# A streamed multiply-and-GELU: the stretch of DRAM loaded first and stored last goes from 5 KB rows to 16 KB rows

## The chip, the cores and the metric

The kernel runs on one core of a Trainium2 chip. The metric is the device time of one execution in microseconds (us), the median of several runs. The engines that matter here are VectorE (DVE in the profile), ScalarE (ACT), SyncE (SP), which issues nearly all transfers, and the 16 DMA engines, which move all bytes between DRAM and the on-chip memory SBUF.

## The reference

Two arrays of 1024 x 4096 float32 are multiplied, and the tanh form of GELU is taken of the product. Each element is independent of all others.

```python
z = x * y
return 0.5 * z * (1 + tanh(sqrt(2 / pi) * (z + 0.044715 * z ** 3)))
```

Each array has 16.78 MB, so 33.55 MB are read and 16.78 MB are written. The kernel computes in float32 throughout.

## The kernel before

**Layout.** SBUF has 128 partitions. The kernel looks at each array as one flat run of 4,194,304 elements and deals out 32,768 of them to each partition. An element keeps no fixed place in a matrix: since the operation is elementwise, any assignment will do as long as x, y and out use the same one. The flat run is cut into three stretches, `PIECES` (line 14). Within a stretch of w columns the helper `columns` (line 51) gives partition p the w consecutive elements that begin at p * w. One transfer therefore moves 128 rows, each contiguous in DRAM, and the row length is 4 * w bytes: 5,120 bytes for the stretch of 1,280 columns, 65,536 for 16,384 columns and 60,416 for 15,104 columns. I call the stretches S (small, first in DRAM), M (middle) and L (last).

**Buffers.** `xs` holds all 32,768 columns of x; products and results overwrite it in place. `ys` holds only 20,440 columns (`Y_BUF`, line 22), so y comes in three loads that share the room. `Y_LOADS` (line 16) lists them as (first column, end, place in `ys`): M at 4056, then L at 0, then S at 15104. Loads L and S overwrite places that products over M must have read before, and `Y_FREE` (line 18) says how many products must be done: 3 for L, 4 for S.

**Order of the transfers.** x of S is issued by SP and x of M by ScalarE's queue, both placed ahead of the kernel's opening barrier by `_hoist` (lines 79 and 80). SP then waits until x of S has landed (line 81) and issues y of M and x of L. It waits for three products and issues y of L, waits for four and issues y of S (lines 84 to 87). After that come the three stores, M, L and S, in the loop at line 111. Each waits until ScalarE has finished its last column (line 114); the first one also waits for a further semaphore (line 113), before: the landing of y of L. All of SP's transfers go through one queue in the order of issue; ScalarE's queue has the one load of x of M. All transfers of both queues share the same 16 DMA engines.

**Compute.** VectorE multiplies in the order of `Y_LOADS`, in steps of `STEPS` (line 20): four steps of 4,096 columns over M, seven of 2,048 and one of 768 over L, one of 1,280 over S. Ahead of the first step of each stretch it waits for the landing of that stretch of x and of y (lines 92 to 95). Each step is followed by one ScalarE activation over the same columns (line 106), which waits for that step (line 105). `done` keeps the number of the step that ends at a column, and line 114 uses it.

**End.** SP waits for the first two stores, clears the semaphores, and waits for the last store (lines 116 to 121).

Of the kernel before, what the change touches and what calls it, by code (L numbers as in the profile page):

```python
# [1 line left out]

# [4 lines left out]

F32 = mybir.dt.float32
GELU = mybir.ActivationFunctionType.Gelu_apprx_tanh  # L10

PIECES = [(0, 1280), (1280, 17664), (17664, 32768)]

Y_LOADS = [(1280, 17664, 4056), (17664, 32768, 0), (0, 1280, 15104)]

Y_FREE = [0, 3, 4]

STEPS = [[4096] * 4, [2048] * 7 + [768], [1280]]  # L20
STORES = [(1280, 17664), (17664, 32768), (0, 1280)]
Y_BUF = 20440

def _hoist(nc, issued):

    here = nc.cur_bb.bb.instructions
    first = nc.main_func.blocks[0].instructions
    for ins in issued:
        del here[next(k for k, i in enumerate(here) if i is ins or i.name == ins.name)]  # L30
    engine = issued[0].engine
    at = next(
        k
        for k, i in enumerate(first)
        if i.engine == engine and type(i).__name__ == "InstDrain"
    )
    first[at:at] = issued

@with_exitstack  # L40
def kernel(
    ctx: ExitStack,
    tc: tile.TileContext,
    x: bass.AP,
    y: bass.AP,
    out: bass.AP,
):
    nc = tc.nc
    P = nc.NUM_PARTITIONS

    def columns(t, a, b):

        flat = t.flatten_outer_dims().rearrange("r c -> (r c)")
        pa, pb = next(q for q in PIECES if q[0] <= a and b <= q[1])
        return flat[P * pa : P * pb].rearrange("(p c) -> p c", p=P)[:, a - pa : b - pa]

    tc.close()
    tc.compile()  # L59

    xs = nc.alloc_sbuf_tensor("xs", [P, PIECES[-1][1]], F32).ap()
    ys = nc.alloc_sbuf_tensor("ys", [P, Y_BUF], F32).ap()
    sem_x = [nc.alloc_semaphore(f"sem_x{i}") for i in range(len(PIECES))]
    sem_y = [nc.alloc_semaphore(f"sem_y{i}") for i in range(len(Y_LOADS))]
    sem_mul = nc.alloc_semaphore("sem_mul")
    sem_act = nc.alloc_semaphore("sem_act")
    sem_o = [nc.alloc_semaphore(f"sem_o{i}") for i in range(len(STORES))]

    def load_x(i, engine=nc.sync):
        a, b = PIECES[i]  # L70
        return engine.dma_start(out=xs[:, a:b], in_=columns(x, a, b)).then_inc(sem_x[i], 16)

    def load_y(i):
        a, b, r = Y_LOADS[i]
        return nc.sync.dma_start(
            out=ys[:, r : r + b - a], in_=columns(y, a, b)
        ).then_inc(sem_y[i], 16)

    _hoist(nc, [load_x(0).ins])
    _hoist(nc, [load_x(1, nc.scalar).ins])  # L80
    nc.sync.wait_ge(sem_x[0], 16)
    load_y(0)
    load_x(2)
    for i in range(1, len(Y_LOADS)):
        if Y_FREE[i]:
            nc.sync.wait_ge(sem_mul, Y_FREE[i])
        load_y(i)

    n = 0
    done = {}  # L90
    for i, (a, b, r) in enumerate(Y_LOADS):
        for j, (xa, xb) in enumerate(PIECES):
            if xa <= a < xb:
                nc.vector.wait_ge(sem_x[j], 16)
        nc.vector.wait_ge(sem_y[i], 16)  # L95
        c = a
        for w in STEPS[i]:
            nc.vector.tensor_mul(  # L98
                out=xs[:, c : c + w],
                in0=xs[:, c : c + w],  # L100
                in1=ys[:, r + c - a : r + c - a + w],
            ).then_inc(sem_mul, 1)
            n += 1
            done[c + w] = n
            nc.scalar.wait_ge(sem_mul, n)
            nc.scalar.activation(  # L106
                out=xs[:, c : c + w], in_=xs[:, c : c + w], func=GELU
            ).then_inc(sem_act, 1)
            c += w

    for i, (a, b) in enumerate(STORES):
        if i == 0:
            nc.sync.wait_ge(sem_y[-2], 16)
        nc.sync.wait_ge(sem_act, done[b])
        nc.sync.dma_start(out=columns(out, a, b), in_=xs[:, a:b]).then_inc(sem_o[i], 16)
    for i in range(len(STORES) - 1):
        nc.sync.wait_ge(sem_o[i], 16)
    nums = sorted(s.num for s in [*sem_x, *sem_y, *sem_o[:-1], sem_mul, sem_act])
    assert nums == list(range(nums[0], nums[-1] + 1))
    nc.sync.sem_clear(range(nums[0], nums[-1] + 1))  # L120
    nc.sync.wait_ge(sem_o[-1], 16).then_inc(sem_o[-1], -16)

# [1 line left out]
_INS = ['x', 'y']  # L125
_OUTS = [((1024, 4096), 'float32')]

# [23 lines left out]
```

## Time and profile before

| what | value |
|---|---|
| median of 3 runs | 119.83 us (119.79 to 119.85) |
| span of the profiled execution, first to last instruction | 118.52 us |
| difference between the two | 1.31 us |
| VectorE busy, 13 products | 35.2 us (30%) |
| ScalarE busy, 13 activations and a table load | 31.0 us (26%) |
| bytes moved, mean rate over the span | 50.33 MB, 425 GB/s |
| DMA packets | 1296 |
| share of the 16 DMA engines' span taken by packets | 82.2% (SP's queue) + 16.5% (ScalarE's queue) |

No time of the profiled execution itself is listed beside its span; the median of the three runs is the nearest thing, and 1.31 us of it lie outside the span.

The 1296 packets are nine transfers of 144. A transfer has 128 data packets, one for each partition's row, and 16 completion packets of 4 bytes, one for each DMA engine, so that each engine moves eight rows of each transfer. The trace keeps a record of every packet (start, duration, size, queue), and the transfer's landing is the arrival of the sixteenth completion. Instructions on SP that issue a transfer are shown as SPq; their landing is given as the time from issue.

### The profile page before, as it was taken

Reading aid. Unit: us, or ns where it says so; the run is one execution under the profiler, and the core shown is the slowest. Engines: PE = TensorE matmul, PEld = TensorE weight load, DVE = VectorE, ACT = ScalarE, POOL = GpSimd, SP = SyncE. Lnnn points to the kernel's source line nnn. Section 1 sums busy time; section 2 is a strip of 40 time slices with the busy share of each in tenths; the row PEclk is TensorE's granted clock in tenths of the full one; section 3 lists DMA queues with packets and bytes.
Section 4 is the critical chain, followed back from the end, with each engine's and each line's share of the span. In section 5 each row is a group of like instructions: output and inputs, shape, how many; then the busy total and the mean of one; then the engine's idle time right before and its main releaser. Section 6 shows DMA issues by size and latency. Waiting matters only on the chain.

```text
span 118.5 us, 82 instructions
## 1 busy us (share of the span) xinstructions
DVE 35.2 (30%) x13; ACT 31.0 (26%) x14; POOL 0.2 (0%) x4
## 2 busy tenths in 40 slices
DVE  0000000000000069999920000059999940000000
ACT  4000000000000000977975000006998990000000
POOL 0000000000000000000000000000000000000000
DMA  9888899889988897797797797798899887977975
GB/s 492 382 382 382 354 575 487 354 354 398 664 354 354 354 652 326 326 652 326 326 632 347 326 632 347 326 575 354 354 531 531 354 354 326 652 326 326 652 326 221
DMA packets 1296, 50.33 MB, mean 425 GB/s; under 512 B 144, under 2 KB 144, under 8 KB 528
## 3 DMA queue, kind: packets, MB, share of 16 engines
q1 hardware_dynamic: 1152, 41.94, 82.2%
q10 hardware_dynamic: 144, 8.39, 16.5%
HBM read 33.55 MB, written 16.78 MB: 425 GB/s over the span
## 4 chain that ended last, share of the span: by engine, by line
DMA 55%; DVE 24%; ACT 3%; issue 1%; DVEq 0%
DMA ys<-in_y_dram 43%; DVE xs L98 24%; DMA xs<-in_x_dram 11%; ACT xs L106 3%; DVEq L95 0%
## 5 line engine op out<-in xcount | busy, mean ns | idle before, releaser
L98 DVE TENSOR_TENSOR xs<-xs,ys 128x2048 f32<-128x2048 f32 (+3 forms) x13 | 35.2, 2777 | 60.9 <-DMA ys<-in_y_dram 60.9
L106 ACT ACTIVATE xs<-xs 128x2048 f32<-128x2048 f32 (+3 forms) x13 | 29.7, 2301 | 65.1 <-DVE xs L98 65.1
L106 ACT ACT_TABLE_LOAD x1 | 1.3, 1283 | 1.6 <-PEq L59 1.6
L136 POOL MEMSET const-bfloat16-1.0<- 128x1 bf16 x1 | 0.1, 103 | 0.0
L136 POOL MEMSET const-uint8-127<- 128x1 uint8 x1 | 0.1, 102 | 0.0
L136 POOL MEMSET const-float32-0.0<- 128x1 f32 x1 | 0.1, 100 | 0.2 <-issue 0.2
L136 POOL MEMSET const-float32-1.0<- 128x1 f32 x1 | 0.1, 99 | 0.0
## 6 DMA issues: line engine op xcount, KB each, us to landing
xs<-in_x_dram SPq DMA_DIRECT2D x1, 7552.0 KB, 46.5
ys<-in_y_dram SPq DMA_DIRECT2D x1, 7552.0 KB, 22.5
out_dram<-xs SPq DMA_DIRECT2D x1, 7552.0 KB, 20.4
xs<-in_x_dram SPq DMA_DIRECT2D x1, 640.0 KB, 13.6
ys<-in_y_dram SPq DMA_DIRECT2D x1, 640.0 KB, 19.7
out_dram<-xs SPq DMA_DIRECT2D x1, 640.0 KB, 20.8
xs<-in_x_dram ACTq DMA_DIRECT2D x1, 30.4
ys<-in_y_dram SPq DMA_DIRECT2D x1, 29.0
```

What stands on the lines that cost most here:

```text
L98: nc.vector.tensor_mul(out=xs[:, c : c + w], in0=xs[:, c : c + w], in1=ys[:, r + c - a : r + c - a + w],).then_inc(sem_mul, 1)
L106: nc.scalar.activation(out=xs[:, c : c + w], in_=xs[:, c : c + w], func=GELU).then_inc(sem_act, 1)
L136: nc = _bacc.Bacc("TRN2", target_bir_lowering=False, num_devices=1)
```

## The change

The stretch S grows from 1,280 to 4,096 columns (rows of 16,384 bytes), M keeps 16,384 columns (65,536 bytes) and moves up in DRAM, and L shrinks from 15,104 to 12,288 columns (rows of 49,152 bytes). The loads, the places in `ys`, the product steps and the stores follow. The last steps of the compute are now six of 2,048 over L, and 2,048, 1,280 and 768 over S. The number of products, of activations and of transfers is the same, and so is the order of the transfers. `Y_FREE` is not changed. The further wait of the first store is now for the fifth product, the first one over L, in place of the landing of y of L.

```diff
-PIECES = [(0, 1280), (1280, 17664), (17664, 32768)]
+PIECES = [(0, 4096), (4096, 20480), (20480, 32768)]
 
-Y_LOADS = [(1280, 17664, 4056), (17664, 32768, 0), (0, 1280, 15104)]
+Y_LOADS = [(4096, 20480, 4056), (20480, 32768, 0), (0, 4096, 12288)]
 
 Y_FREE = [0, 3, 4]
 
-STEPS = [[4096] * 4, [2048] * 7 + [768], [1280]]
-STORES = [(1280, 17664), (17664, 32768), (0, 1280)]
+STEPS = [[4096] * 4, [2048] * 6, [2048, 1280, 768]]
+STORES = [(4096, 20480), (20480, 32768), (0, 4096)]
 Y_BUF = 20440
...
     for i, (a, b) in enumerate(STORES):
         if i == 0:
-            nc.sync.wait_ge(sem_y[-2], 16)
+            nc.sync.wait_ge(sem_mul, len(STEPS[0]) + 1)
         nc.sync.wait_ge(sem_act, done[b])
```

## The prediction

> **What bounds the kernel now.** I read the summary page first, for the engines and the DMA.
>
> ```profile
> span 118.5 us, 82 instructions
> DVE 35.2 (30%) x13; ACT 31.0 (26%) x14; POOL 0.2 (0%) x4
> ...
> DMA packets 1296, 50.33 MB, mean 425 GB/s; under 512 B 144, under 2 KB 144, under 8 KB 528
> ...
> q1 hardware_dynamic: 1152, 41.94, 82.2%
> q10 hardware_dynamic: 144, 8.39, 16.5%
> ```
>
> No compute engine is busy for a third of the span, and packets fill 82.2 + 16.5 = 98.7% of the 16 DMA engines' span. 1.3% of 118.5 us, some 1.5 us, is all that the DMA engines do not use, and 1.0 us of that is the time before the first packet. So no edit can win much unless packets get cheaper, and an edit loses whatever idle time it opens on all DMA engines.
>
> The packet records tell whether packets get cheaper. A row of 5,120 bytes takes 196 ns (median), one of 60,416 bytes 2,229, one of 65,536 bytes 2,418. The two large ones fit 7 ns a packet plus 0.0368 ns a byte, and the small one does too (188 + 7 = 195). The change keeps 72 data packets on each DMA engine and the same bytes, so the sum of packet times is unchanged: 7 + 603 = 610 ns for 16,384 bytes and 7 + 1,809 = 1,815 for 49,152 make 2,425, as 196 + 2,229 do. **The row length by itself costs or brings nothing.**
>
> The Trainium skill, page "DMA: Bandwidth & Descriptors", section on measured bandwidth, would have it otherwise: transfers should have at least 1 MiB for 75% of peak, and it gives 341 GB/s for 1 MB. By it the three small transfers of 0.66 MB would take 1.92 us each or more, and an estimate of 3 x (1.92 - 1.54), 1.1 us, could be won by the growth. The rows here disagree: eight such packets take 1.57 us on each engine, 418 GB/s, back to back with the next transfer. In the other direction, the same page's row on HBM row pitch at large powers of two gives 207 in place of 214 GB/s at a pitch of 512 KiB; if that held at 16 KiB, it would be an estimated 0.5 us on the three new transfers. The 65,536-byte rows here, a power of two as well, load at the same cost per byte as the 60,416-byte ones, and no row of 16 KiB is in this trace.
>
> What is left is the order in time. The chain of waits shows it:
>
> ```profile
> 0.00 13.55 DMA xs<-in_x_dram
> 13.55 0.02 issue
> 13.57 28.99 DMA ys<-in_y_dram
> ...
> 42.66 13.11 DVE xs L98 x3
> 55.76 0.02 issue
> 55.78 22.47 DMA ys<-in_y_dram
> 78.25 0.03 issue
> ```
>
> Each "issue" here is a place where SP had to wait before it could give the DMA engines more work. They are three: y of M after x of S (13.57), y of L after the third product (55.78), and the store of M after y of L (78.27, 0.02 after the landing). At each the question is whether the queues still hold work. The table of issues gives the landings:
>
> ```profile
> xs<-in_x_dram SPq DMA_DIRECT2D x1, 7552.0 KB, 46.5
> ys<-in_y_dram SPq DMA_DIRECT2D x1, 7552.0 KB, 22.5
> ...
> xs<-in_x_dram ACTq DMA_DIRECT2D x1, 30.4
> ys<-in_y_dram SPq DMA_DIRECT2D x1, 29.0
> ```
>
> x of L was issued at 13.96 and lands 46.5 later, at 60.4. So y of L, issued at 55.78, stands in the queue 4.6 us before the load ahead of it lands. That is today's cover at the second place, and the change eats it.
>
> **Step 1, y of L is asked for later.** Ahead of y of M's landing each DMA engine must now move x of S, x of M and y of M with eight rows of S that are longer by 610 - 196 = 414 ns: y of M lands 8 x 0.414 = 3.31 us later, at 42.56 + 3.31 = 45.87. `Y_FREE` still asks for three products (three steps over M free places up to 4056 + 3 x 4096 = 16,344; two would free 12,248, 40 short of the 12,288 that y of L needs now). The 13.11 us of those products follow, so y of L is issued at 55.78 + 3.31 = 59.09. x of L in front of it starts 3.31 later and is 3.31 shorter, so it ends when it did. By the packet records the 16 engines complete it between 59.50 and 60.02 us. So the engines run dry 0.41 to 0.93 us after the issue, and what counts is how long an issued transfer takes to bring its first bytes.
>
> Two rows bound this. The store of M, issued at 78.27, brought its first packets on waiting engines at 79.11 to 79.22: 0.84 to 0.95 us. The first load, issued at 0.00 into empty engines, has its first packets starting from 1.01; taking 196 ns off their ends, data flowed from 1.25 to 1.63 us. On the slowest engine, which alone sets the end, the loss is therefore 0.95 - 0.93 = 0.02 us by the store's row and 1.63 - 0.93 = 0.70 us by the load's. The engines that finish x of L early wait longer, but that only takes away their lead. The first row is the nearer in state (SP in the middle of the kernel, 328 to 348 ns to issue), the second in kind (a read of DRAM into empty engines). The first packets of x of M, a load that came to engines at work, took 0.15 us over the usual 2.418 in the mean and 0.26 at most, so a load's first packet does cost more than a store's (0.03 over). I take the middle, **+0.37 us**.
>
> **Step 2, y of M is asked for later.** x of S shares the engines with x of M, one packet of each queue by turns once both are there: before, five rows of S went ahead, then one 65,536-byte packet for each further row and one ahead of the completion, four in all. With rows of 610 ns about two go ahead (the first x of M packets came at 2.30 to 2.62), and seven packets of x of M come ahead of the completion of S. That puts it near 2.8 + 7 x 2.42 + 6 x 0.61 = 23.4 us on an engine, the landing at some 24. One packet of x of M, 2.42 us, then remains as cover. The completion takes 0.36 to reach SP (13.19 to 13.55), and the first bytes 0.84 to 1.63: 1.2 to 2.0, inside 2.42. Cost taken: nothing. With five ahead as before the cover is four packets. If only one row of S went ahead, the cover would be gone and the cost 1.2 to 2.0 us.
>
> **Step 3, the store of M.** Before, its issue came so late that engines done with y of S at 78.89 stood idle till 79.11. In the window 78.9 to 79.2 the packets leave 0.09 us empty in the mean, but the last engine, done at 79.38, waited for nothing. After, y of S takes 8 x 0.610 = 4.88 us in place of 1.57. The new wait, the fifth product, comes 2.29 + 0.1 us after the landing of y of L (the first 128x2048 product after the wait took 2.293), that is about 2.8 after its last packet, and with 0.95 for the first bytes 3.7 of the 4.88 us are used. The idle time goes; worth 0 to 0.09, I take 0. What is late next is nothing: the stores of L and S wait for activations, whose 2,048-column steps run at 2.20 us and end some 3 us earlier than before, while the store of M keeps the queue busy for 19.4 us.
>
> **Step 4, compute.** The steps over L and S have the same shapes in another order (7 x 2048, 1280, 768), 18.2 us of products on an engine with slack. Nothing. No queue of another engine is passed; POOL has no transfer.
>
> **Sum.** 0.37 + 0 + 0 + 0 on the profiled span of 118.52 makes 118.9; with the 1.31 us between span and median, 120.2 us, +0.3%. About 0.2% (0.24 us) is what a measurement of this kernel can tell from no change.
>
> **The rivals.**
>
> The cover suffices. If the first bytes of y of L arrive as the store's did, the slowest engine loses 0.02 and the result is 119.8 to 120.0. For it: the issue leads by 0.93, the store needed 0.95. Against it: x of S's first packets.
>
> Starved at the start (step 2 gone wrong). x of M is used up when y of M is issued; all engines stand for 1.2 to 2.0 us; with step 1's loss this gives 121.4 to 122.2. It decides if ScalarE's transfer gets its first turn straight after the first row of S. Against it: five to six rows went ahead before, and the second row of S would start by about 2.2, ahead of the 2.30 at which x of M came.
>
> Faster: a smoother start. On the slowest engine the completion of x of S came at 13.19, although its eight rows and the four packets of x of M need only 8 x 0.196 + 4 x 2.418 = 11.24 us; data flowed from 1.25 us on the earliest engine, so 0.69 us were lost on the ramp, part of it in first packets of x of M that were up to 0.26 long. If 610-ns rows give those requests time to run ahead, the price is at most -0.69; half of it with step 1 at 0.02 gives 119.5. It decides only if it brings 0.24 more than step 1 costs.
>
> The change not doing what it says is excluded: the order of instructions shows the new shapes on each queue.
>
> **How the numbers follow.** Forecast case (step 1 costs over 0.24): 0.58, 120.2 us. Cover suffices, or a small loss and the ramp cancel: 0.25. Starved at the start: 0.08. Faster start: 0.09. Slower is 0.58 + 0.08 = 0.66, same 0.25, faster 0.09. The forecast's own bounds are 119.85 to 120.53; 0.15 for first packets of x of M going either way, and part of the same-time rival, make the range 119.75 to 120.8. It leaves out the starved start and most of the faster one.
>
> **What would show it.** In the profile after: the issue of y of L at about 59.1, the landing of x of L still at 60.4 or so; the landing of y of L at 75.3, while without a gap it would be at 60.02 + 14.52 + 0.37 = 74.9; packets absent from most engines just before and after 60; the store of M issued 2.4 us after the landing of y of L, with no idle engine at y of S's end. A landing of x of S beyond 24.5 with idle engines near 26 would speak for the starved start. The forecast is wrong if the packets of 16,384 bytes do not take 610 ns, or if the DMA engines carry on across 60 us without a gap on the last of them.

## The result and the profile after

The changed kernel takes 121.82 us (median of 5 runs, 121.73 to 122.02) against 119.83 before on the same chip: a ratio of 1.0164, 95% interval 1.0149 to 1.0179, so 2.0 us slower. The forecast was 120.2 (119.75 to 120.8). The direction was right, the size was not.

The page of the changed kernel, the lines that answer to those of before:

```profile
span 120.7 us, 82 instructions
DVE 35.2 (29%) x13; ACT 31.0 (26%) x14; POOL 0.2 (0%) x4
...
DMA packets 1296, 50.33 MB, mean 417 GB/s; under 512 B 144, under 2 KB 144, under 8 KB 144
...
q1 hardware_dynamic: 1152, 41.94, 81.8%
q10 hardware_dynamic: 144, 8.39, 16.1%
```

Work, bytes and packets are the same. The two shares of the DMA engines' span, 97.9%, are of a span that is 2.2 us longer, so packet time grew as well: 118.05 us for each DMA engine in the mean by the packet records, 116.98 before. Half of the loss is idle time, half is packets that took longer. Of the 1.1 us that the engines are idle more, 0.58 lie around 60 us and 0.54 at the end, where the engines that finish early wait for the last one (last completions from 119.30 to 120.31, before from 117.95 to 118.11). The chain of waits (start, duration, what) says where to look:

```profile
0.00 24.10 DMA xs<-in_x_dram
24.10 0.02 issue
24.12 22.10 DMA ys<-in_y_dram
...
46.32 13.11 DVE xs L98 x3
59.42 0.02 issue
59.44 17.66 DMA ys<-in_y_dram
77.10 0.03 issue
```

y of M lands at 46.22, y of L is asked for at 59.44, both within 0.35 us of what was worked out. But y of L then lands at 77.10, not at 75.3. The table of issues for the same transfers:

```profile
xs<-in_x_dram SPq DMA_DIRECT2D x1, 6144.0 KB, 36.2
ys<-in_y_dram SPq DMA_DIRECT2D x1, 6144.0 KB, 17.7
```

x of L, issued at 24.50, lands at 60.7, 0.3 us later than before. From there on y of L with its 6.3 MB is alone on the DMA engines, and it needs until 77.1. A table of stretches around 60 us shows the stop. The last two columns are the DMA share and GB/s; a packet is counted whole in the stretch where it starts, so a stretch in which all engines begin a long packet shows far over 1. First the kernel before:

```profile
59.50:60.00 0.50, 0.50 (x1) 0.00 (x0) 0.00 (x0) 1.00 4.21 1813
60.00:60.50 0.50, 0.09 (x1) 0.38 (x1) 0.00 (x0) 1.00 0.28 121
```

Then the changed one:

```profile
59.50:60.00 0.50, 0.50 (x1) 0.50 (x1) 0.00 (x0) 1.00 0.01 0
60.00:60.50 0.50, 0.50 (x1) 0.50 (x1) 0.00 (x0) 1.00 1.79 492
60.50:61.00 0.50, 0.50 (x1) 0.50 (x1) 0.00 (x0) 1.00 3.30 983
```

Before, the engines go from x of L straight to y of L between 59.5 and 60. After, they complete x of L between 59.77 and 60.36 (the share of 0.01 is the completion packets), and their first packets of y of L start between 60.40 and 61.20. And these first packets are long: 2,657 ns in the mean and 3,499 at most, where a 49,152-byte packet takes 1,815 ns once the transfer runs.

The last completion on any engine, transfer by transfer, makes the account (us; "worked out" is before plus the packet times of the change):

| last completion of | before | worked out | after | added here |
|---|---|---|---|---|
| y of M | 42.19 | 45.50 | 45.86 | 0.36 |
| x of L | 60.02 | 60.03 | 60.36 | -0.03 |
| y of L | 77.83 | 74.56 | 76.76 | 1.87 |
| y of S | 79.38 | 79.46 | 81.62 | -0.04 |
| store of S | 118.11 | 118.19 | 120.31 | -0.04 |

Nearly all of the loss arises in two places, 0.36 us where y of M begins and 1.87 us where y of L begins. In the mean of the 16 engines the second is 1.43 us: 0.58 idle and 0.86 in longer packets. The last engine loses 0.45 more, since the completions, which lay within 0.60 us of each other for x of L, lie 1.24 us apart for y of L.

### The profile page after: what moved, and what is told of

Its sections match the earlier page's. It is cut to its first block, busy times and chain, and to the rows that moved or that the text cites. A ratio compares the mean times of both kernels' runs of the same rounds, so it can differ in the third digit from the quotient of the medians.

```text
span 120.7 us, 82 instructions
## 1 busy us (share of the span) xinstructions
DVE 35.2 (29%) x13; ACT 31.0 (26%) x14; POOL 0.2 (0%) x4
## 4 chain that ended last, share of the span: by engine, by line
DMA 53%; DVE 22%; ACT 3%; issue 2%; DVEq 0%
DMA ys<-in_y_dram 33%; DVE xs L98 22%; DMA xs<-in_x_dram 20%; ACT xs L106 3%; DVEq L95 0%
## 6 DMA issues: line engine op xcount, KB each, us to landing
ys<-in_y_dram SPq DMA_DIRECT2D x1, 2048.0 KB, 18.2
```

## The experiments

**Theory A:** y of L (and a little y of M) is asked for too late; the queue runs out, and taking the flow up again is slow. **Theory B:** the new row lengths, 16 KB and 48 KB, or their pitch in DRAM, are slower in themselves. "Lead" below is the time from the issue of y of L to the last completion of x of L, 0.92 us in the changed kernel and 4.24 in the one before. "Loss on the last engine" is the step of the last completion from x of L to y of L, less eight packets (14.53 us with 48 KB rows). All ratios are to the kernel before on the same chip.

### Asking for y of L earlier (e1_early_yl)

```diff
-STEPS = [[4096] * 4, [2048] * 6, [2048, 1280, 768]]
+STEPS = [[4136, 4096, 4096, 4056], [2048] * 6, [2048, 1280, 768]]
-Y_FREE = [0, 3, 4]
+Y_FREE = [0, 2, 4]
```

> Changed kernel, but y of L is asked for after two products in place of three (the first step over M is 4,136 columns wide, so two steps free the 12,288 places). Its issue moves from 59.4 to about 55.1 us, 5 us ahead of the end of x of L. Theory A (the queue runs dry at 60 us and the restart is slow): the idle stretch and the long first packets of y of L vanish, worth 1.88 us on the last engine (16.40 in place of 14.52 us for eight 48 KB rows); median about 119.9 to 120.1. Theory B (rows of 16 KB or 48 KB, or their pitch in DRAM, are slower in themselves): the idle 0.56 us goes, but the rest of the loss stays; about 121.3.

120.16 us, ratio 1.0024 (1.0015 to 1.0032), 0.06 above theory A's range and far from theory B's 121.3. Its chain:

```profile
46.26 8.81 DVE xs L98 x2
55.07 0.02 issue
55.09 20.14 DMA ys<-in_y_dram
75.23 0.03 issue
```

The wait is for two products, the issue at 55.09, and y of L lands at 75.23, 1.87 us earlier than in the changed kernel although the x of L ahead of it lands at the same time (60.70 against 60.74). The stretches around 60 us:

```profile
59.50:60.00 0.50, 0.50 (x1) 0.50 (x1) 0.00 (x0) 1.00 1.60 688
60.00:60.50 0.50, 0.50 (x1) 0.50 (x1) 0.00 (x0) 1.00 2.06 885
```

In no half microsecond between 2 and 117 us are the engines less than 97% busy, 48 KB packets take 1,816 ns in the mean, and the loss on the last engine is nil. 40 columns, by which two products missed the room for y of L, decided 1.66 of the 1.99 us.

### No wait for x of S (e2_no_start_wait, e3_both)

```diff
-    nc.sync.wait_ge(sem_x[0], 16)
     load_y(0)
```

The second version also has the edit of e1_early_yl.

> Changed kernel without SP's wait for x of S (line 81), which only holds back the issue of y of M; VectorE still waits for x of S itself. Theory A: the first rows of y of M no longer begin straight after the last row of x of M with 2.5 to 3.0 us in place of 2.42; the 0.34 us by which y of M comes later than worked out go, and the stop at 60 us stays: about 121.5. Theory B: the start is not at fault; 121.8 as before.

> Both edits: y of L asked for after two products, and no wait for x of S. Theory A: all of the loss goes, 1.88 + 0.34 = 2.2 us; 119.6 to 119.9, no idle stretch between 1.5 us and the end, and packets of 48 KB at 1,815 ns throughout. Theory B: above 121 us, with 16 KB and 48 KB packets above 610 and 1,815 ns while no queue is empty.

Both edits: 120.01 us, ratio 1.0010 (1.0001 to 1.0019), 0.1 above theory A's range. The first packets of y of M take 2,418 ns where they took 2,690 in the mean (3,020 at most) in the changed kernel, y of M completes at 45.54 (worked out: 45.50), and the last store packet is over at 118.12, before: 118.12. Rows of 16 KB and 48 KB run at 611 and 1,815 ns in the middle of the flow. Theory B falls: with both requests early, the new rows cost 0.1% (0.2% at the upper end of the interval), and the larger transfers bring nothing either.

Taking out the wait alone (e2_no_start_wait) gave 122.09 us, not 121.5. The start did improve as expected (y of M completes 0.31 us earlier), but the stop at 60 us was still there and cost 2.09 us on the last engine in place of 1.87. Why the median is 0.27 us above that of the changed kernel is not shown; the profiled execution has a span 0.1 us shorter (120.58 against 120.68).

### The same fault put into the kernel before (e4_before_late_yl)

```diff
-Y_FREE = [0, 3, 4]
+Y_FREE = [0, 4, 4]
```

> Kernel before (rows of 5 KB, 60 KB and 64 KB), but y of L is asked for after four products in place of three: issue at about 60.1 us in place of 55.8, when x of L ends between 59.5 and 60.0. Theory A: the stop is no matter of the new row lengths; about 0.1 us late plus 1.6 to 2.8 us till the first packets run at full rate gives 121.5 to 122.7, with the first packets of y of L far over 2,229 ns. Theory B (the restart is cheap with the old rows, first bytes after 0.95 us): 120.9.

122.58 us, ratio 1.0219 (1.0195 to 1.0244), inside theory A's range. With 5, 60 and 64 KB rows the issue comes 0.10 us after the last completion of x of L, and the last engine loses 2.44 us. Its chain:

```profile
42.80 17.44 DVE xs L98 x4
60.25 0.02 issue
60.26 20.54 DMA ys<-in_y_dram
```

From an issue into empty engines to the landing it takes 20.54 us, of which eight packets are 17.84; the first packets start 0.95 to 1.6 us after the issue and take 2,973 ns in the mean in place of 2,229.

### How much lead is enough (e5_lead_2us, e13_lead_3us, e14_lead_4us)

```diff
-STEPS = [[4096] * 4, [2048] * 6, [2048, 1280, 768]]
+STEPS = [[4096, 4096, 3072, 1024, 4096], [2048] * 6, [2048, 1280, 768]]
-Y_FREE = [0, 3, 4]
+Y_FREE = [0, 3, 5]
```

This is e5; the two narrow steps are 2,048 and 2,048 columns wide in e13, 1,024 and 3,072 in e14.

> Changed kernel with the third product of M split into 3,072 and 1,024 columns, so that y of L is asked for 1.1 us earlier: about 2.0 us ahead of the last completion of x of L in place of 0.92. Theory A with the measured restart (the last engine had y of L at full rate 2.80 us after the issue): if the time from issue to full rate stays 2.8 us whatever the queue holds, the last engine still loses 0.8, 120.9 us. If a queue that still holds work hides most of it, as in the case of y of M after x of M, whose first packets were 0.27 us long on average at a lead of 0.7 to 1.1 us, the loss is 0.1 to 0.4: 120.2 to 120.5.

> Changed kernel, third product of M split into 2,048 and 2,048 columns: y of L is asked for 2.2 us earlier, 2.6 to 3.1 us ahead of the completions of x of L. Theory H (a transfer that arrives in the last 3 us or so of the one ahead is taken over badly, however much is left, and smoothly only with more in front): still idle engines and long packets at 60 us, 121 to 123. Theory I (the loss falls steadily with the lead; the run with 2 us was spoilt by something else): 0 to 0.3 us left, 120.0 to 120.4.

> The same with 1,024 and 3,072 columns: y of L is asked for 3.2 us earlier, 3.6 to 4.1 us ahead, as in the kernel before (3.7 to 4.2). Both theories: no gap at 60 us, 120.0 to 120.3. If it is above 120.6, the number of steps or the split itself is what cost time in the runs with a split third product.

| kernel | lead, us | loss on the last engine, us | median, us | runs, us |
|---|---|---|---|---|
| e4_before_late_yl | -0.10 | 2.44 | 122.58 | 122.24 to 122.83 |
| changed kernel | 0.92 | 1.87 | 121.82 | 121.73 to 122.02 |
| e5_lead_2us | 1.93 | 1.32 | 122.32 | 121.67 to 123.18 |
| e13_lead_3us | 3.00 | 0.76 | 121.23 | 120.86 to 121.55 |
| e14_lead_4us | 4.13 | -0.03 | 120.22 | 120.03 to 120.37 |
| e1_early_yl | 5.24 | -0.02 | 120.16 | 120.04 to 120.27 |

Ratios: 1.0227 (1.0188 to 1.0266) for the lead of 1.93 us, 1.0107 (1.0082 to 1.0133) for 3.00, 1.0025 (1.0013 to 1.0036) for 4.13. In these profiled executions the loss falls by some 0.55 us for each us of lead and is gone between 3.0 and 4.1. The medians do not show so steady a fall. The profiled executions of e5 and e13 were the fastest of four (121.67 and 120.86), and by the medians the time above e1_early_yl is 1.66 us at a lead of 0.92, 2.16 at 1.93, 1.07 at 3.00 and 0.06 at 4.13. Both cases of the expectation for e5 missed. For e13 theory H's range came, and theory I's 120.0 to 120.4 did not. Splitting the product costs nothing (e14). With 3 us the transfer is issued while more than one packet is still ahead of it on each engine (x of L completes 2.48 to 3.00 us after the issue), and yet its first packets take 1,965 ns in the mean, 2,601 at most. The chain of e13:

```profile
46.30 10.97 DVE xs L98 x3
57.28 0.02 issue
57.30 18.64 DMA ys<-in_y_dram
```

### A later store with that lead (e11_lead_2us_late_store)

By theory A alone, the lead of 1.93 us should not have a higher median than one of 0.92. I suspected the first store.

```diff
-STEPS = [[4096, 4096, 3072, 1024, 4096], [2048] * 6, [2048, 1280, 768]]
+STEPS = [[4096, 4096, 3072, 1024, 4096], [3072, 1024] + [2048] * 4, [2048, 1280, 768]]
```

> The version with y of L asked for 2.0 us ahead (122.32 us, 121.67 to 123.18), and the first product over L 3,072 columns wide, so that the first store is issued about 1.1 us later (80.0). Theory M: the scatter and the time above 121.2 of that version came from its store meeting loads; now 121.0 to 121.6 and a narrow scatter (the first engines to end y of S stand for up to 1.3 us, the last one does not). Rival: the scatter is that of the restart itself; again around 122.3.

122.87 us, 1.0250 (1.0233 to 1.0267). The runs lie close together (122.71 to 123.05), as theory M said, but 1.3 us above its range, and the loss is at 60 us, ahead of the store: y of L was issued at 58.40 as in e5_lead_2us, and the last engine lost 2.38 us there in place of 1.32. The store came only at 81.11 (80.0 was worked out) and left the engines idle for another 1.1 us in the mean around 81 us. Up to the issue of y of L the two programs are the same, so at 2 us of lead the handover from x of L to y of L itself varies between executions (these two were on different chips). At a lead of 0.9 us the changed kernel, e2 and e6 lost 1.87, 2.09 and 1.99. What decides the length of the handover is open.

### Shorter rows first (e7_split_5k, e8_split_24k)

```diff
+        if i == 1:
+            m = a + 1280
+            nc.sync.dma_start(
+                out=ys[:, r : r + m - a], in_=columns(y, a, m)
+            ).then_inc(sem_y[i], 16)
+            a, r = m, r + m - a
...
-        nc.vector.wait_ge(sem_y[i], 16)
+        nc.vector.wait_ge(sem_y[i], 32 if i == 1 else 16)
```

In e8 the first part has 6,144 columns.

> Changed kernel, y of L asked for at the same time but as two transfers, the first of 1,280 columns (rows of 5,120 bytes), the second of the rest. Theory P (a long row is what makes the restart slow: the first packets of all engines start together and each runs slow for its whole length): 5 KB rows had the first load at full rate 1.25 to 1.63 us after its issue, so the last engine gains about 1.2 us, less 0.07 for the extra packets: about 120.7. Theory L (a fixed time till the full rate, or a loss of the same size spread over more packets): 121.8 to 122.0.

> As the run with 5,120-byte rows first, with two equal halves of 6,144 columns (rows of 24,576 bytes). Theory P: between the 16 KB rows of the first load (1.3 to 1.9 us from issue to full rate) and the 48 KB rows (1.6 to 2.8), some 2.2 on the last engine: gain about 0.6, 121.3. Theory L: 121.8 to 122.0.

121.53 us (ratio 1.0141, 1.0126 to 1.0156) and 121.97 (1.0182, 1.0158 to 1.0206). The first is 0.3 us faster than the changed kernel, the second 0.15 slower: theory P's gains of 1.2 and 0.6 us did not come. Take the completion of the restarted transfer less its eight packets as the moment of full rate. Counted from the issue, the first engine is there after 1.62, 1.52 and 1.55 us with rows of 5, 24 and 48 KB, whatever their length; the last engine after 2.24, 2.58 and 2.79. So on the first engine, and for most of the time on the last, the row length makes no difference. Whether the rest grows with it is not shown: rows of 60 KB had their last engine there after 2.35 us (e4_before_late_yl).

### The wait of the first store (e12_before_new_store_wait, e6_old_store_wait, e9_early_yl_old_store_wait, e10_before_no_store_wait)

The other part of the change, by itself on the kernel before:

```diff
-            nc.sync.wait_ge(sem_y[-2], 16)
+            nc.sync.wait_ge(sem_mul, len(STEPS[0]) + 1)
```

> Kernel before with the wait edit alone: the first store waits for the fifth product. With only 1.57 us of y of S behind y of L the queue runs dry: the store is issued at about 80.65 in place of 78.27, its first packets come 0.84 to 0.95 later, at 81.5 to 81.6, and the last engine is done with y of S at 79.38: about 2.2 us longer, 122.0 to 122.1. Rival (the cover is elsewhere): 119.9.

122.30 us, 1.0204 (1.0187 to 1.0221), 0.2 above what was worked out. The stores on SP's queue (start, duration, what), first in the kernel before and then here:

```profile
78.27 19.77 SPq L115 DMA_DIRECT2D out_dram<-xs  x3
```

```profile
80.70 17.54 SPq L115 DMA_DIRECT2D out_dram<-xs  x3
```

The first store is issued at 80.70, the last engine was done with the loads at 79.43, and the engines idle for 2.5 us in the mean between 79 and 82 us. A store, unlike a load, has no long first packets: they start 0.84 to 0.99 us after the issue and take 2,458 ns in the mean, 1.6% over the usual. The reverse, the old wait in the changed kernel and in e1_early_yl:

> Changed kernel with the first store waiting for the landing of y of L again, as before the change. The last engine did not wait there in the changed kernel (y of S ends at 81.62, the store of M had been there since 80.6), so theory A: no change, 121.7 to 122.0. Rival: the new wait takes part in the loss; then up to 0.2 us less.

> The version with y of L asked for after two products (120.16 us), with the first store waiting for the landing of y of L as before the change: the store is issued at about 75.3 us in place of 77.6, when 3.9 to 4.4 us of loads are still ahead of it in the queue. Theory M (a store that is queued behind loads still at work makes their packets slow, as the 16 KB packets of y of S after 78.4 us in the run with the old wait): those packets again take 700 to 1,300 ns in place of 611, and the time is about 1.5 us longer, 121.6. Rival N (they were slow only because the engines had been set apart by the restart at 60 us): no change, 120.0 to 120.3.

123.38 us (1.0298, 1.0267 to 1.0329) and 120.91 (1.0090, 1.0075 to 1.0105), so 1.56 and 0.75 us worse than with the new wait. For e6 both expectations were wrong: theory A had no change, and the rival had a gain. For e9 it is theory M, though with half the price it gave. The table of issues of e9, and then of e1, shows it in y of S:

```profile
ys<-in_y_dram SPq DMA_DIRECT2D x1, 2048.0 KB, 17.0
```

```profile
ys<-in_y_dram SPq DMA_DIRECT2D x1, 2048.0 KB, 16.4
```

Both are issued at 63.8 or 63.7. 39 of the 128 packets of y of S took over 650 ns in e9, up to 1,213, from 1.5 us after the issue of the store; none did in e1, where the store comes 2.3 us later. To see how far this goes, the kernel before without any further wait:

```diff
-        if i == 0:
-            nc.sync.wait_ge(sem_y[-2], 16)
```

> Kernel before without the further wait of the first store (line 113): the store of M is issued when its activations are done, at about 63.8 us, behind all of y of L and y of S in the same queue. Theory M: the packets of y of L are slow from about 65 us on; some 13 us of loads at 10 to 40% more, 1.5 to 5 us, so 121 to 125. Rival N: a queue is a queue; the idle 0.09 us before the store goes, 119.7 to 119.9.

120.92 us, 1.0092 (1.0076 to 1.0107), in neither range. The store stands in the queue from 63.85 on, and yet y of L runs at 2,232 ns until 75.1; only the last packets of the loads are slow, seven of y of L and 84 of 128 of y of S (311 ns in the mean in place of 196). Theory M as I had put it, a slowdown as long as the store stands there, is wrong. What these runs show is narrower: where loads run out with a store already behind them, the packets of the last 3.6 to 5.3 us of loads are slow, at a price of 0.75 to 1.56 us, and a store that is issued 1.6 to 2.1 us ahead of the last load's end (e1: 77.64, loads over at 79.19 to 79.70) costs nothing. The mechanism inside the DMA engines is open.

## Why the prediction was wrong

**Packet costs: right.** 16,384 bytes take 611 ns (610 worked out) and 49,152 bytes 1,815 (1,815). Bytes and packets give back what they take, as e3_both shows with 120.01 against 119.85 us. The gain that the rule on transfers of 1 MiB would give (the Trainium skill, page "DMA: Bandwidth & Descriptors", section on measured bandwidth) did not come: three transfers that grew from 0.66 to 2.10 MB brought nothing. The page's figures there are for transfers issued from GpSimd; here SP issues them, each behind another in the queue, and which of the two matters is not shown. A row pitch of 16 or 48 KiB cost nothing at these sizes.

**Step 1: place and cause right, size wrong, and this is the step that failed.** The move of y of M's landing, the third product, the issue of y of L (59.09 worked out, 59.44 measured) and x of L's end were as written. The term "+0.37 us" measured 1.87. It priced only the wait for the first bytes, and let the packets after that run at their usual time; in the mean of the engines the idle time was 0.58 us, and 0.86 more went into packets that took longer. It took the time from issue to first bytes from two rows, 0.95 us for a store and 1.25 to 1.63 for the first load, and put the middle between them. The store's row does not hold for loads: a load into empty engines in the middle of the kernel reached full rate after 1.55 us on the first engine and 2.79 on the last. The first load's row was nearer, but it was read at the start of the kernel, and only as far as the first bytes. And "only takes away their lead" was too kind: the engines do not restart together, and their completions, 0.60 us apart for x of L, were 1.24 apart for y of L. One reading was also a little off, without effect: the first packets of x of M took 0.13 us over the usual in the mean, not 0.15. The Trainium skill, page "DMA: Bandwidth & Descriptors", section on latency and other measured facts, gives about 600 ns to the first byte for a transfer issued from SP; here the first packets start 0.95 us after the start of the issuing instruction (e4, and 0.96 in the changed kernel). Counted from its end, 0.33 us later, that is 0.62 and 0.63 us, which agrees with the page. The full rate comes much later, after 1.55 us or more.

**Step 2: "cost taken: nothing" measured 0.36.** The order of packets was as worked out, x of S landed at 24.10 (24 worked out), and no engine stood still. But the 1.6 to 2.0 us of cover were not enough: the first packets of y of M took 2,690 ns in place of 2,418. It is a late request as in step 1, and an earlier one removes it (e3_both). But the price at one lead differs by place: 0.36 us here, with 1.59 to 2.04 us of work ahead, and 1.32 and 2.38 for y of L in e5 and e11 with 1.28 to 1.98 (the expectation for e5 gives y of M 0.7 to 1.1, which is what is left after 0.95 us to the first packets). Here the packets ahead were of ScalarE's queue, there of SP's own; whether that is the reason is not shown. The range of the rival "starved at the start", 121.4 to 122.2, holds the result, but by accident: no engine starved there. Nor did the rival of a smoother start bring anything: with the request early, y of M completes at 45.54, and 45.50 was worked out without such a gain (e3_both).

**Step 3: right for the changed kernel, for one reason too few.** The wait edit cost nothing there: the store was issued 2.42 us after the landing of y of L (2.4 worked out), and the last engine did not wait. But the prediction saw only a choice between idle time and none. The edit alone on the old sizes costs 2.4 us (e12), and the old wait with the new sizes 1.56 us (e6): the wait and the size of S belong together, and a store that comes too early has a price too.

**Step 4: right.** Products and activations have slack throughout. (The products over L and S take 17.8 us, not 18.2, which changes nothing.)

**The range.** Its upper end was the worst of the rows shown (0.70) and 0.27 more. Neither row showed a load's restart in the middle of the kernel, and such a cost, that no row shows, should have had a wider upper end.

## What to carry to other kernels

Where the DMA engines are the bound, count for each transfer how many us of queued work are still ahead of it when it is issued. For y of L in this kernel, 4.1 us were enough and 3.0 were not; less cost up to 2.4 us at that one place, and it began to cost before the queue was empty. The idle time of the engines is not the whole price of a late load: in the changed kernel longer first packets and engines that no longer ran in step made up 1.3 of the 1.87 us. When a buffer is resized, recompute which step frees the room for the next load: 40 columns too many moved a request by 4.3 us.

## What the runs showed that I had not expected

- A load's first packets can be long even when it is issued before the queue is empty: with 3.0 us of lead still 1,965 ns in the mean for 1,815 (e13), with 4.1 no longer (e14).
- Stores and loads ask for opposite care. A store restarts at close to the full rate 0.84 to 0.99 us after its issue (e12), but if it stands behind loads that are running out, the last of these take up to 2.2 times as long with 16 KB rows (e6, e9, e10: 0.75 to 1.56 us in all).
- At a lead of 2 us the same program varied from 121.67 to 123.18 us (e5), where the kernel before stayed within 0.4 us over 21 runs on one chip. That variation is not explained.
